# A hybrid decoder layer: 16 of 22 K tiles of the down projection as seven half products, low weight parts last, pairs begun with the weights' sums, nine weight slots

## The chip, the cores and the metric

The kernel runs on one core of a Trainium2 chip. The metric is the device time of one execution in microseconds (us), taken as the median over runs. Engines are named as in the profile: PE (TensorE), DVE (VectorE), ACT (ScalarE), POOL (GpSimd) and SP (SyncE, which issues DMAs).

## The reference, cut to what matters

One layer: a combined input projection, three recurrent branches, a merge, and a SwiGLU feed-forward block (FFN) between RMSNorms. 512 prompt columns and 64 sample columns are computed together, 576 in all, which the kernel holds as two halves of 288. D_MODEL is 1024 (8 tiles of 128), D_FF is 2816 (22 tiles).

```python
h = rmsnorm(x, g_pre_mix)
z = h @ w_in                      # x-branch, gates, S5 input, q, k, v, decays, merge gates
merged = sum(sigmoid(gate_b) * y_b for b in (rglru, s5, gated_delta))
x1 = x + rmsnorm(merged @ w_out, g_post_mix)
h2 = rmsnorm(x1, g_pre_ffn)
act = silu(h2 @ w_gate) * (h2 @ w_up)          # 22 tiles of 128 rows
y = x1 + rmsnorm(act @ w_down, g_post_ffn)
```

## The kernel before

Every product is made in split precision: weight and activation are each kept as a high part (fp32r) and a low part, and one K tile of 128 costs three matmuls of 128x128 by 288 columns: hi by x-hi, hi by x-lo, lo by x-hi. In a GEMM (`mm_part`, lines 210 to 218) these three stand side by side for each K tile; `mm3` takes both halves in turn, weight tile by weight tile, into two accumulators in PSUM.

Weights come from DRAM as raw float32. `wsplit` makes the parts with ACT (a copy to fp32r, L198) and DVE (raw minus hi, L199). `wsplit_dma` makes them with ACT alone (hi, L181, and minus hi, L182) and lets an accumulating DMA, issued by POOL, add the raw weight from DRAM to the low part (L183).

The FFN's gate and up tiles m = 0 to 3 are plain GEMMs. Tiles 4 to 21 are made in pairs, gate pair and up pair for each two tiles, by `pair`: a 2x2 block product with seven half products instead of eight, each a `product` of 4 K tiles (12 matmuls), 84 matmuls a pair. `pair_w` fetches two raw blocks of 512 KB (SP, L1446) and makes from them four sums or differences of weights on DVE (L1452, L1453, L1454, L1459) and seven split weights: three (w0, w1, w6) by DMA, four (w2 to w5) by DVE. DVE also adds the products up (L1482 to L1493) and applies the gate. The activations' sums for this were made before the stage.

`down` multiplies K tiles in groups of four behind the pairs of m = 4, 8, 12 and 16: 8 weights split by DVE, 192 matmuls and 16 evictions (L1519 adds to the accumulator `mx`, the tile `xr`). `down(16, 2)` and a final stage of 4 K tiles end the FFN; the final stage takes half 0 over all 8 output tiles, then half 1, squares and sums for the norm (L1551 eviction, L1557 add), scales (L1561), adds x1 (L1562) and stores y.

What sets the order: every engine runs its instructions in a fixed order, which a scheduler derives from the program's order with priorities (weight preparation is raised by `tc.high_priority`). Buffers recur through pools: raw blocks in 2 + 2 slots, split weights in 4 + 4 slots (`ff_alloc` alternates between the pools `wp` and `sx`), PSUM accumulators in a ring of banks.

```python
def ff_alloc(c):
    wqn[0] += 1
    return two(wp, "wh", "wl")(c) if wqn[0] % 2 else two(sx, "wh", "wl", bufs=4)(c)
```

## Time and profile before

| | |
|---|---|
| median of 3 runs | 1096.17 us (1094.71 to 1105.67) |
| the profiled execution | 1094.42 us |
| its span in the profile | 1092.5 us |
| PE busy | 1041.3 us, 95% |
| DVE busy | 779.0 us, 71% |
| ACT busy | 510.5 us, 47% |
| POOL busy | 167.4 us, 15% |
| mean granted TensorE clock | 0.967 |

The span is what the trace shows between first and last instruction; the execution's time has some 2 us around it. Busy shares are means over stages: the FFN's pairs and down groups run from about 726 to 1052 us. A duration of a matmul (0.3 us) is longer than the step from one to the next, since they are pipelined; the step is read from starts. In a row of the timeline the bracket at the end is the idle time of the engine ahead of the instruction and what ended it.

### The profile page before, as it was taken

Reading aid. Unit: us, or ns where it says so; the run is one execution under the profiler, and the core shown is the slowest. Engines: PE = TensorE matmul, PEld = TensorE weight load, DVE = VectorE, ACT = ScalarE, POOL = GpSimd, SP = SyncE. Lnnn points to the kernel's source line nnn. Section 1 sums busy time; section 2 is a strip of 40 time slices with the busy share of each in tenths; the row PEclk is TensorE's granted clock in tenths of the full one; section 3 lists DMA queues with packets and bytes.
Section 4 is the critical chain, followed back from the end, with each engine's and each line's share of the span. In section 5 each row is a group of like instructions: output and inputs, shape, how many; then the busy total and the mean of one; then the engine's idle time right before and its main releaser. Section 6 shows DMA issues by size and latency. Waiting matters only on the chain.

```text
span 1092.5 us, 20102 instructions
## 1 busy us (share of the span) xinstructions
PE 1041.3 (95%) x7658; PEld 992.8 (91%) x7658; DVE 779.0 (71%) x1893; ACT 510.5 (47%) x1041; POOL 167.4 (15%) x224
## 2 busy tenths in 40 slices
PE   8889898899999999999899999899999999999994
PEld 6788897899999989998699999899999999999994
DVE  7988888646898769844637647874676766857756
ACT  5368667445444423332233535355654635635620
POOL 1132211110120210011000031200211201112124
PEclk9999997699999999999799999999999999999997
DMA  6656664362323133222112622144673736636602
GB/s 210 170 122 143 146 140 98 77 179 88 102 82 107 45 129 119 85 54 97 40 54 74 235 78 75 42 108 118 128 188 75 185 98 136 181 91 145 155 1 87
DMA packets 75138, 122.58 MB, mean 112 GB/s; under 512 B 28186, under 2 KB 36642, under 8 KB 75042
## 3 DMA queue, kind: packets, MB, share of 16 engines
q1 hardware_dynamic: 61938, 97.44, 28.2%
q0 software_dynamic: 13104, 23.86, 13.7%
q8 instruction: 60, 0.98, 0.4%
q14 instruction: 36, 0.29, 0.1%
HBM read 113.03 MB, written 8.24 MB: 111 GB/s over the span
## 4 chain that ended last, share of the span: by engine, by line
PE 73%; DVE 9%; DMA 6%; issue 6%; ACT 3%; POOL 1%; SPq 1%; DVEq 0%; POOLq 0%; ACTq 0%
PE mm L216 13%; PE mm L218 13%; PE mm L217 12%; PE mm L1470 8%; PE mm L1468 8%; PE mm L1469 8%; DMA wl<-in_w_in 2%; DVE wl L199 1%; PE up L1225 1%; DMA wl<-in_w_gate 1%; PE xp L690 1%; DMA wr<-in_w_in 1%; DMA wr<-in_w_gate 1%; PE kp L1036 1%; PE zq L1207 1%
## 5 line engine op out<-in xcount | busy, mean ns | idle before, releaser
L216 PE MATMUL mm<-hh,wh 128*128 128x288 f32 x768 | 231.5, 304 | 3.6 <-DVE u L417 2.3
L198 ACT ACTIVATE wh<-wr 128x512 fp32r<-128x512 f32 x213 | 131.9, 629 | 218.5 <-PE mm L217 118.7
L218 PE MATMUL mm<-hh,wl 128*128 128x288 f32 x768 | 230.3, 301 | 3.5 <-DMA wl<-in_w_in 3.5
L217 PE MATMUL mm<-hl,wh 128*128 128x288 f32 x768 | 230.7, 301 | 0.0
L199 DVE TENSOR_TENSOR wl<-wr,wh 128x512 fp32r<-128x512 f32 x213 | 146.4, 695 | 72.9 <-ACT wh L198 67.2
L216 PEld LDWEIGHTS mm<-hh,wh 128*128 128x128 f32 x768 | 145.9, 191 | 8.4 <-issue 4.8
L218 PEld LDWEIGHTS mm<-hh,wl 128*128 128x128 f32 x768 | 146.2, 191 | 6.8 <-DMA wl<-in_w_in 4.2
L217 PEld LDWEIGHTS mm<-hl,wh 128*128 128x128 f32 x768 | 146.2, 191 | 4.2 <-issue 3.7
L1470 PE MATMUL mm<-fh,wl 128*128 128x288 f32 x352 | 103.8, 295 | 0.0
L1468 PE MATMUL mm<-fh,wh 128*128 128x288 f32 x320 | 94.8, 297 | 0.1
L1469 PE MATMUL mm<-fl,wh 128*128 128x288 f32 x320 | 94.3, 295 | 0.0
L181 ACT ACTIVATE wh<-wr 128x512 fp32r<-128x512 f32 x91 | 56.9, 628 | 78.1 <-PE mm L1469 44.9
L1470 PE MATMUL mm<-hfh,wl 128*128 128x288 f32 x288 | 84.7, 297 | 1.0 <-DMA wl<-in_w_gate 0.9
L1468 PE MATMUL mm<-hfh,wh 128*128 128x288 f32 x288 | 84.8, 295 | 0.0
L1469 PE MATMUL mm<-hfl,wh 128*128 128x288 f32 x288 | 84.8, 295 | 0.0
L216 PE MATMUL mm<-brh,wh 128*128 128x288 f32 x224 | 67.5, 308 | 1.6 <-DVE mg L843 0.9
L217 PE MATMUL mm<-brl,wh 128*128 128x288 f32 x224 | 68.7, 308 | 0.2 <-DVE rho L714 0.2
L218 PE MATMUL mm<-brh,wl 128*128 128x288 f32 x224 | 68.4, 307 | 0.0
L1470 PEld LDWEIGHTS mm<-fh,wl 128*128 128x128 f32 x352 | 66.1, 188 | 0.0
L1469 PE MATMUL mm<-t,wh 128*128 128x288 f32 x216 | 64.0, 297 | 0.0
L1470 PE MATMUL mm<-t,wl 128*128 128x288 f32 x216 | 63.7, 295 | 0.0
L1468 PE MATMUL mm<-t,wh 128*128 128x288 f32 x216 | 63.6, 295 | 0.0
(505 smaller groups left out, 2592.7 us busy)
## 6 DMA issues: line engine op xcount, KB each, us to landing
wr<-in_w_in SPq DMA_DIRECT2D x48, 512.0 KB, 3.5
wr<-in_w_gate SPq DMA_DIRECT2D x22, 512.0 KB, 3.9
wr<-in_w_up SPq DMA_DIRECT2D x22, 512.0 KB, 3.8
wr<-in_w_down SPq DMA_DIRECT2D x20, 512.0 KB, 4.7
wl<-in_w_in POOLq DMA_DIRECT2D x30, 256.0 KB, 5.5
wl<-in_w_gate POOLq DMA_DIRECT2D x27, 256.0 KB, 4.5
wl<-in_w_up POOLq DMA_DIRECT2D x27, 256.0 KB, 4.4
wr<-in_w_out SPq DMA_DIRECT2D x8, 512.0 KB, 3.5
```

Source lines behind the costliest of these rows:

```text
L181: S.activation(hi, raw, AF.Copy)
L198: S.activation(hi, raw, AF.Copy)
L199: (eng or lo_eng()).tensor_tensor(lo, raw, hi.bitcast(F32), op=OP.subtract)
L216: PE.matmul(acc, hi[:, k, :], xh[:, sl], start=k0 + k == 0, stop=False)
L217: PE.matmul(acc, hi[:, k, :], xl[:, sl], start=False, stop=False)
L218: PE.matmul(acc, lo[:, k, :], xh[:, sl], start=False, stop=k0 + k == n - 1)
L690: PE.matmul(xpv[:, b_, :], gm[g // 4][:, g % 4, :], x[:, g, :], start=True, stop=True)
L1036: PE.matmul(kp[:, b], k2[:, sl], kqe[:, :, sl], start=True, stop=True)
L1207: PE.matmul(zqv[:, b], s0[:, b, :], kqe[:, :, c0:c0 + 8], start=True, stop=True)
L1468: PE.matmul(acc, hi[:, k0 + k, :], xh, start=new and k == 0, stop=False, skip_group_check=not new)
L1469: PE.matmul(acc, hi[:, k0 + k, :], xl, start=False, stop=False, skip_group_check=not new)
L1470: PE.matmul(acc, lo[:, k0 + k, :], xh, start=False, stop=k == len(x) - 1, skip_group_check=not new)
```

## The change

1. `product` and the GEMMs (`mm_parts` in place of `mm_part`) issue all hi matmuls of a product first and the matmuls with the low weight part last.
2. `pair` takes its products in the order w2, w3, w0, w4, w1, w5, w6 (before: w0, w2, w3, w4, w1, w5, w6).
3. Split weights have nine slots in place of eight (4 in `wp`, 5 in `sx`).
4. Down of K tiles 0 to 15 is made by `down7`, as seven half products over 2x2 blocks as well: 168 matmuls a group in place of 192, with weights packed on the host (`w_down7`), prepared by `pair_w` as gate and up are, three of seven low parts by DMA. The activations' differences and their splits are made by `down_x0` and `down_x1` (4 differences and 7 splits of 128x576 per group, in place of 4 splits). 28 accumulations a group in place of 16. One term that all pairs of rows share (`ut`) is added once at the end by a broadcast.
5. To make room, x1 is stored to DRAM (`x1d`) and read back for the last step; the activation ring has 3 tiles, one of which lies in the new accumulator tile `fa`, as do the pair's temporaries.
6. The final stage has 6 K tiles (`NL`) in place of 4, and `down(16, 2)` goes.
7. In the last step all adds of squares are on DVE, and half 0's adds of x1 too (before: POOL).

PE's order holds 7042 matmuls before the change and 6946 with it.

```diff
-                PE.matmul(acc, hi[:, k, :], xh[:, sl], start=k0 + k == 0, stop=False)
-                PE.matmul(acc, hi[:, k, :], xl[:, sl], start=False, stop=False)
-                PE.matmul(acc, lo[:, k, :], xh[:, sl], start=False, stop=k0 + k == n - 1)
+    def mm_parts(ps, ws, x, halves, after=None):
+        n = len(x)
+        for lo_part in range(2):
+            k0 = 0
+            for w in ws:
+                for acc, half in zip(ps, halves):
...
+                            if lo_part:
+                                PE.matmul(acc, w[1][:, k, :], xh[:, sl], start=False, stop=k0 + k == n - 1)
+                            else:
+                                PE.matmul(acc, w[0][:, k, :], xh[:, sl], start=k0 + k == 0, stop=False)
+                                PE.matmul(acc, w[0][:, k, :], xl[:, sl], start=False, stop=False)
...
+        SY.dma_start(x1d[:, :, sl], x1t[:, :, sl])
...
-        return two(wp, "wh", "wl")(c) if wqn[0] % 2 else two(sx, "wh", "wl", bufs=4)(c)
+        return two(wp, "wh", "wl")(c) if wqn[0] % 9 in (1, 3, 5, 7) else two(sx, "wh", "wl", bufs=5)(c)
...
         for k, (xh, xl) in enumerate(x):
-            PE.matmul(acc, hi[:, k0 + k, :], xh, start=new and k == 0, stop=False, skip_group_check=not new)
-            PE.matmul(acc, hi[:, k0 + k, :], xl, start=False, stop=False, skip_group_check=not new)
-            PE.matmul(acc, lo[:, k0 + k, :], xh, start=False, stop=k == len(x) - 1, skip_group_check=not new)
+            PE.matmul(acc, hi[:, k0 + k, :], xh, start=new and k == 0, stop=False, skip_group_check=skip)
+            PE.matmul(acc, hi[:, k0 + k, :], xl, start=False, stop=False, skip_group_check=skip)
+        for k, (xh, _) in enumerate(x):
+            PE.matmul(acc, lo[:, k0 + k, :], xh, start=False, stop=k == len(x) - 1 and not more, skip_group_check=skip)
...
+        S.activation(u, product(ws[2], 0, hx[2]), AF.Copy)
+        pz = product(ws[3], 0, hx[3])
         px = product(ws[0], 0, hx[0])
-        S.activation(u, px, AF.Copy)
-        V.tensor_tensor(u, u, product(ws[2], 0, hx[2]), op=OP.add)
-        pz = product(ws[3], 0, hx[3])
+        V.tensor_tensor(u, u, px, op=OP.add)
...
+    def down_x0(k0):
+        t = act2(k0)
+        b11, b12 = (t[:, :, hsl(b)] for b in range(2))
+        dx[0] = fparts(b11)
+        V.tensor_tensor(b11, b12, b11, op=OP.subtract)
+        dx[3] = fparts(b11)
+
+    def down_x1(k0):
+        b11, b12, b21, b22 = quarters(k0)
+        V.tensor_tensor(b12, b22, b12, op=OP.subtract)
+        dx[4] = fparts(b12)
+        dx[5] = fparts(b22)
+        V.tensor_tensor(b22, b22, b11, op=OP.subtract)
+        dx[2] = fparts(b22)
+        dx[1] = fparts(b21)
+        V.tensor_tensor(b21, b21, b22, op=OP.subtract)
+        dx[6] = fparts(b21)
...
+    def down7(k0):
+        c = k0 == 0
+        for g in range(2):
+            ws = pair_w(i["w_down7"], k0 + 2 * g)
+            for e in range(2):
+                p_ = 2 * g + e
+                q = 2 * e
+                u = ut[:, p_, :]
+                c1, c2 = mx[2 * p_], mx[2 * p_ + 1]
+                add_to(u, product(ws[2], q, dx[2]), c)
+                pz = product(ws[3], q, dx[3])
+                add_to(c2[:, hsl(1)], pz, c)
+                px = product(ws[0], q, dx[0])
+                V.tensor_tensor(u, u, px, op=OP.add)
+                pw_ = product(ws[4], q, dx[4])
+                V.tensor_tensor(c2[:, hsl(1)], c2[:, hsl(1)], pw_, op=OP.add)
+                product(ws[1], q, dx[1], px)
+                add_to(c1[:, hsl(0)], px, c)
+                product(ws[5], q, dx[5], pz)
+                add_to(c1[:, hsl(1)], pz, c)
+                product(ws[6], q, dx[6], pw_)
+                add_to(c2[:, hsl(0)], pw_, c)
...
+        if k0 is not None:
+            down_x1(k0)
         pair(i["w_up"], m, lambda a, sl, c: glu_u(t[:, a, sl], c))
...
+        if k0 is not None:
+            down7(k0)
...
-                (V if half and m > 3 else G).tensor_tensor(ss, ss, sq, op=OP.add)
+                V.tensor_tensor(ss, ss, sq, op=OP.add)
...
-            (V if half and m in (3, 5, 7) else G).tensor_tensor(xv, xv, x1[m][:, sl], op=OP.add)
+            (V if half == 0 or m in (3, 5, 7) else G).tensor_tensor(xv, xv, x1[m][:, sl], op=OP.add)
```

In the changed file the matmuls of a GEMM are L226, L227 (hi) and L224 (low), those of a product L1479, L1480 (hi) and L1482 (low); the weights' sums are L1462, L1463, L1464 and L1469; the split by DVE is L200 for weights and L260 for activations; `down7`'s accumulations L1548 to L1565; the last step L1623 (eviction), L1629, L1633, L1634.

**PE where the first pair begins.** Before: the last GEMM of the plain tiles ends (L216 to L218), and the first product takes the weight wh_8682 with its low part wl_8683 from the third matmul on; the names are accumulator<-activation part, weight part.

```order
L218 MATMUL mm_8628<-hfh_7415,wl_8143 128x288
L216 MATMUL mm_8628<-hfh_7417,wh_8142 128x288
L217 MATMUL mm_8628<-hfl_7418,wh_8142 128x288
L218 MATMUL mm_8628<-hfh_7417,wl_8143 128x288
L1468 MATMUL mm_8720<-hfh_7403,wh_8682 128x288
L1469 MATMUL mm_8720<-hfl_7404,wh_8682 128x288
L1470 MATMUL mm_8720<-hfh_7403,wl_8683 128x288
L1468 MATMUL mm_8720<-hfh_7405,wh_8682 128x288
L1469 MATMUL mm_8720<-hfl_7406,wh_8682 128x288
```

Of the change, the same place: the GEMM ends in eight matmuls on low parts, and the first product is on wh_8686, with its two last rows here repeated three times more, eight matmuls without a low part.

```order
L224 MATMUL mm_8616<-hfh_7411,wl_8143 128x288
L224 MATMUL mm_8616<-hfh_7413,wl_8143 128x288
L224 MATMUL mm_8616<-hfh_7415,wl_8143 128x288
L224 MATMUL mm_8616<-hfh_7417,wl_8143 128x288
L1479 MATMUL mm_8713<-t_1450_8424,wh_8686 128x288
L1480 MATMUL mm_8713<-t_1451_8425,wh_8686 128x288
```

The low part has moved behind, and the first weight is another one: wh_8686 is the hi part of w2, wh_8682 and wh_8678 (further on in the change) those of w0.

**DVE around a weights' sum in a cycle of the middle.** Before: L1452 makes the sum ws_10377 from a raw block; L1482 to L1486 evict products, L199 are splits of the weights of the pair before.

```order
L1454 TENSOR_TENSOR wr_10224<-ws_10228,wr_10224 128x512
L1452 TENSOR_TENSOR ws_10377<-wr_10375 128x512
L254 TENSOR_TENSOR fl_10077<-ar_9524,fh_10076 128x576
L1482 TENSOR_TENSOR cu_10121<-cu_10121,mm_10138 128x288
L199 TENSOR_TENSOR wl_10238<-wr_10224,wh_10237 128x512
L1453 TENSOR_TENSOR wr_10375<-wr_10373,wr_10375 128x512
L199 TENSOR_TENSOR wl_10242<-ws_10228,wh_10241 128x512
L1484 TENSOR_TENSOR c_1723_10123<-cu_10121,mm_10152 128x288
L199 TENSOR_TENSOR wl_10246<-wr_10226,wh_10245 128x512
L1486 TENSOR_TENSOR c_1723_10123<-c_1723_10123,mm_10166 128x288
L1459 TENSOR_TENSOR wr_10224<-wr_10224 128x512
L1400 SCALAR_TENSOR_TENSOR ar_10080<-ar_10080,mm_10124 128x288
```

Of the change, the like place, with the sum ws_10001 (L1462); L1538 is a difference of activations, L260 a split of one, L1504 and L1507 evictions of a pair.

```order
L1462 TENSOR_TENSOR ws_10001<-wr_9999 128x512
L1538 TENSOR_TENSOR ar_8206<-ar_8206,fa 128x2x288
L1408 SCALAR_TENSOR_TENSOR ar_8207<-ar_8207,mm_9618 128x288
L200 TENSOR_TENSOR wl_9865<-wr_9851,wh_9864 128x512
L1463 TENSOR_TENSOR wr_9999<-wr_9997,wr_9999 128x512
L1504 TENSOR_TENSOR fa<-fa,mm_9605 128x288
L260 TENSOR_TENSOR fl_9702<-ar_8206,fh_9701 128x576
L1507 TENSOR_TENSOR fa<-fa,mm_9633 128x288
L200 TENSOR_TENSOR wl_9869<-ws_9855,wh_9868 128x512
L260 TENSOR_TENSOR fl_9706<-ar_8206,fh_9705 128x576
L200 TENSOR_TENSOR wl_9873<-wr_9853,wh_9872 128x512
L1497 TENSOR_TENSOR fa<-fa,mm_9781 128x288
```

More rows stand behind the sum that were not there before: differences and splits of 128x576 and, five rows further on, the first eviction of `down7` (L1548, mm_9891).

**DVE in the last half.** Before: an eviction (L1551), the scaling of half 0 (L1561, 8 rows), then evictions and three adds of squares.

```order
L1551 TENSOR_TENSOR xr<-xr,mm_12788 128x288
L1561 SCALAR_TENSOR_TENSOR xr<-xr,par,rows_12710 128x288 x8
L1551 TENSOR_TENSOR xr<-xr,mm_12805 128x288
L1551 TENSOR_TENSOR xr<-xr,mm_12822 128x288
L1551 TENSOR_TENSOR xr<-xr,mm_12839 128x288
L1557 TENSOR_TENSOR fs_12752<-fs_12752,fs_12819 128x288
L1557 TENSOR_TENSOR fs_12752<-fs_12752,fs_12836 128x288
L1557 TENSOR_TENSOR fs_12752<-fs_12752,fs_12853 128x288
L1551 TENSOR_TENSOR xr<-xr,mm_12856 128x288
```

Of the change, the same place: the adds of x1 to half 0 (L1634) stand among the evictions (L1623) and the adds of squares (L1629).

```order
L1633 SCALAR_TENSOR_TENSOR xr<-xr,par,rows_12763 128x288 x8
L1629 TENSOR_TENSOR fs_12811<-fs_12811,fs_12879 128x288
L1634 TENSOR_TENSOR xr<-xr,x_2140_12541 128x288
L1634 TENSOR_TENSOR xr<-xr,x_2141_12542 128x288
L1634 TENSOR_TENSOR xr<-xr,x_2142_12543 128x288
L1634 TENSOR_TENSOR xr<-xr,x_2143_12544 128x288
L1623 TENSOR_TENSOR xr<-xr,mm_12882 128x288
L1634 TENSOR_TENSOR xr<-xr,x_2144_12545 128x288
L1634 TENSOR_TENSOR xr<-xr,x_2145_12546 128x288
L1634 TENSOR_TENSOR xr<-xr,x_2146_12547 128x288
L1634 TENSOR_TENSOR xr<-xr,x_2147_12548 128x288
L1623 TENSOR_TENSOR xr<-xr,mm_12905 128x288
```

Eight rows L1634 have come to DVE ahead of the last evictions.

## Rows read from the trace of the kernel before

**Rows 1.** The page's busy time, share and instructions of each engine.
```profile
PE 1041.3 (95%) x7658; PEld 992.8 (91%) x7658; DVE 779.0 (71%) x1893; ACT 510.5 (47%) x1041; POOL 167.4 (15%) x224
```

**Rows 2.** Busy time of the engines by stretch; the first line names the columns.
```profile
core 0: us, PE busy (x) PEld busy (x) DVE busy (x) ACT busy (x) POOL busy (x), PEclk, DMA share, GB/s
675.00:700.00 25.00, 23.17 (x176) 22.54 (x174) 20.01 (x58) 9.37 (x20) 5.53 (x6) 1.00 0.32 107
175.00:200.00 25.00, 19.66 (x89) 15.48 (x87) 20.46 (x47) 17.10 (x29) 1.04 (x5) 0.60 0.25 54
726.00:1052.00 326.00, 324.91 (x2437) 323.65 (x2437) 225.38 (x423) 169.83 (x309) 46.75 (x55) 1.00 0.55 131
...
792.00:861.00 69.00, 69.00 (x522) 69.00 (x522) 48.20 (x91) 34.59 (x61) 9.55 (x12) 1.00 0.56 133
```

**Rows 3.** DVE's groups, 800 to 1000 us: count, busy us, mean ns, idle before.
```profile
L199 DVE TENSOR_TENSOR wl<-wr,wh 128x512 fp32r<-128x512 f32 x57 | 39.0, 688 | 5.4 <-ACT wh L198 3.7
L1519 DVE TENSOR_TENSOR xr<-xr,mm 128x288 f32<-128x288 f32 x48 | 21.6, 452 | 25.3 <-PE mm L1470 25.2
L254 DVE TENSOR_TENSOR fl<-ar,fh 128x576 fp32r<-128x576 f32 x12 | 9.0, 751 | 0.0
L1452 DVE TENSOR_TENSOR ws<-wr 128x512 f32<-128x512 f32 x12 | 8.3, 693 | 17.7 <-DMA wr<-in_w_gate 12.8 <-DMA wr<-in_w_up 4.8
```

**Rows 4.** PE's timeline, first product of the pairs and two waits (start, us).
```profile
728.36 0.29 PE L1468 MATMUL mm<-hfh,wh 128*128 128x288 f32 x1
...
729.30 0.40 PE L1470 MATMUL mm<-hfh,wl 128*128 128x288 f32 x1 [0.52 <-DMA wl<-in_w_gate]
...
1008.48 0.40 PE L1470 MATMUL mm<-hfh,wl 128*128 128x288 f32 x1 [0.42 <-DMA wl<-in_w_gate]
```

**Rows 5.** PE's timeline in the GEMMs of w_in.
```profile
112.91 0.40 PE L216 MATMUL mm<-hh,wh 128*128 128x288 f32 x1 [0.28 <-ACT pad L453]
...
236.55 0.40 PE L218 MATMUL mm<-hh,wl 128*128 128x288 f32 x1 [1.20 <-DMA wl<-in_w_in]
```

**Rows 6.** DVE's timeline: first sum of weights, an eviction and the next row.
```profile
724.49 0.69 DVE L1452 TENSOR_TENSOR ws<-wr 128x512 f32<-128x512 f32 x1
...
864.19 0.45 DVE L1484 TENSOR_TENSOR c<-cu,mm 128x288 f32<-128x288 f32 x1
864.55 0.69 DVE L199 TENSOR_TENSOR wl<-wr,wh 128x512 fp32r<-128x512 f32 x1
```

**Rows 7.** ACT's timeline, one copy; the page's DMA issues: KB, us to landing.
```profile
845.54 0.63 ACT L181 ACTIVATE wh<-wr 128x512 fp32r<-128x512 f32 x1 [0.95 <-PE mm L1469]
...
wr<-in_w_gate SPq DMA_DIRECT2D x22, 512.0 KB, 3.9
...
wl<-in_w_gate POOLq DMA_DIRECT2D x27, 256.0 KB, 4.5
```

**Rows 8.** PE's and DVE's timelines: release and sum, first and last of 15.
```profile
762.60 0.30 PE L1468 MATMUL mm<-fh,wh 128*128 128x288 f32 x1
...
766.84 0.69 DVE L1452 TENSOR_TENSOR ws<-wr 128x512 f32<-128x512 f32 x1 [5.99 <-DMA wr<-in_w_up]
...
997.23 0.30 PE L1470 MATMUL mm<-hfh,wl 128*128 128x288 f32 x1
...
1005.65 0.69 DVE L1452 TENSOR_TENSOR ws<-wr 128x512 f32<-128x512 f32 x1 [1.80 <-DMA wr<-in_w_up]
```

**Rows 9.** DVE's and PE's timelines at the end.
```profile
1072.98 2.77 DVE L1557 TENSOR_TENSOR fs<-fs,fs 128x288 f32<-128x288 f32 x3
1075.67 0.44 DVE L1551 TENSOR_TENSOR xr<-xr,mm 128x288 f32<-128x288 f32 x1
...
1075.90 0.30 PE L272 MATMUL cps<-con,fs 128*96 128x1 f32 x2 [1.73 <-DVE fs L1557]
...
1085.19 1.88 DVE L1562 TENSOR_TENSOR xr<-xr,x 128x288 f32<-128x288 f32 x3
```

## What the change does to the time: the prediction

> **What bounds the kernel now.** I read the busy shares first: TensorE (PE) is busy 1041.3 of the span of 1092.5 us [rows 1]. [...] So in the FFN a matmul taken away is time taken away, as long as no other engine comes late there. One cycle of that stage (four pairs and one group of down) is the stretch 792 to 861: 522 matmuls in 69.00 us, 0.1322 us each, with DVE at 48.20 us, ACT at 34.59 and POOL at 9.55 [rows 2]. DVE is next in line, 70% busy. The groups of DVE then show what it does there (one 128x512 row takes 0.69 us, an eviction 0.45, a 128x576 row 0.75) and that its idle time stands largely in front of the weights' sums: 17.7 us before 12 of them, released by the raw weights' DMA [rows 3]. The timeline gives the single waits.
>
> The profiled execution took 1094.42 us, 1.75 below the median of the runs (1096.17). The sum is made against 1094.42.
>
> **The change part by part.**
> Matmuls. Four groups of down go from 192 to 168 matmuls each, the rest keeps its count: 96 fewer, at 0.1322 us [rows 2], **-12.7 us**, if nothing is late in their place. [...]
>
> Low parts last. A product that began with hi and lo side by side had to have its low part at the third matmul: PE waited 0.52 us at 729.30 and 0.42 at 1008.48 for one that comes by DMA [rows 4]. Now eight matmuls lie ahead of it, over 1 us: **-0.9**. In the GEMMs of w_in the wait of 1.20 us at 236.55 [rows 5] goes likewise: **-1.2**. Earlier ones lie ahead of the stretch with the clock at 0.60, where PE waits for other engines anyway; I count them at nothing (up to 2 more if that is wrong).
> Against that, in a GEMM of both halves the two accumulators now end four matmuls apart and not twelve, so the first evictions bunch, and a bank of PSUM comes free later for the next GEMM. In the two orders I count 22 places where a bank is wanted less than 2.4 us after its last matmul, against 5. One such wait shows in before, 0.28 us behind an ACT eviction [rows 5]. Bounds: nothing, and 22 x 0.28 = 6. I take **+0.5**, since the evicting engines there are mostly ahead of PE.
>
> Start of the pairs. The first product is now the one on w2, which needs the sum and the two differences and then its split, where w0 needed only a copy. The first sum begins at 724.49 [rows 6]. Six DVE rows and a copy of 0.63 behind it give about 728.8, and PE is ready at about 728.4. With later pairs' first products (traced by hand: 0.5 each for the second pair and the first down) I take **+1.5**, bounds 0 and 3.
>
> The loop of the raw weights. This is the main unknown. A raw block is fetched again only when its last hi copy has a weight slot, and that slot must be freed by PE: ACT's copy (0.63, [rows 7]), SP's issue, the landing (3.9 us at the page's row for gate, [rows 7]), then the sum on DVE. From the freeing matmul to the sum I measured 15 pairs in before: 4.2 us in the first (762.60 to 766.84), 8.4 in the last (997.23 to 1005.65) [rows 8], median 6.2. Behind the sum, on DVE's queue, stand evictions and splits that PE wants. In before nothing is late even at 8.4 us: for the sum ws_10377, whose neighbourhood stands in the order shown with the change, 161 matmuls, 21.3 us, lie between the slot's release and the first matmul that needs what stands behind the sum, and DVE's rows in between take 9.7. In the changed order the like place (ws_10001) has 106 matmuls, 14.0 us, for DVE rows of 9.1: the loop may take 4.9. Summed over the 23 pairs of the changed order by this count, PE is late by 0 at a loop of 4.5 us, 1.2 at 5.5, 4.4 at 6.2, 12.1 at 7.2 and 29.8 at 8.4. I take the median of the measured loops: **+4.4**, bounds 0 and 29.8.
>
> DVE's load. Per cycle come 8 rows of weight sums (8 x 0.69), 7 of 128x576 (4 differences of the activations, 7 splits in place of 4; 7 x 0.75) and 12 evictions (28 for 16; 12 x 0.45) [rows 3]: 16.2 us. 48.20 + 16.2 = 64.4 us in a cycle of 504 matmuls, 66.6 us. It fits, barely: 97% by durations. The durations overlap, though: the eviction at 864.19 has 0.45 and the next row starts 0.36 later [rows 6]; by such steps it is near 90%. Nothing is added for load alone; its price is in the lateness above and in the slow rival below. ACT has 16 more rows a cycle or so and stays near 65%.
>
> DMA'd low parts. Six more accumulating DMAs a cycle (POOL had 12 rows, [rows 2]). Their own loop, copy 0.63, negated copy 0.63, landing 4.5 [rows 7], is 5.8 us; eight weights have slack between 2.8 us and nothing. **+0.8**, bounds 0 and 4. The DMA engines' share is 0.56 there [rows 2], so the transfers, the saved x1 (written and read once) among them, find room.
>
> Tail. In before three adds (L1557) take 2.77 us beside POOL's adds and hold the last eviction to 1075.67; PE waits 1.73 for what follows [rows 9]. Now POOL adds nothing then, but eight adds of half 0 join DVE, 0.63 each by the row at 1085.19 (1.88 for three, [rows 9]), before the last evictions. **-0.5**, bounds -1.2 and +1.4. Two more K tiles in the final stage are matmuls moved, not added. The four broadcast adds lie beside the final weights' products.
>
> Sum: -12.7 - 0.9 - 1.2 + 0.5 + 1.5 + 4.4 + 0.8 - 0.5 = -8.1, so **1086.3 us**.
>
> **The rivals.**
> *Everything is hidden.* Copy and landing alone are 0.63 + 3.9 = 4.5 us [rows 7], and at such a loop nothing is late. Then only the gains stand: 1094.4 - 12.7 - 0.9 - 1.2 - 0.5 = 1079.1. For it: PE was busy 324.91 of 326 us with loops up to 8.4. Against: the margin shrinks from 11.6 to 4.9 us in the example, below the median loop.
> *Slower: DVE's sum blocks its queue.* Place: the weights' sum in the six pairs of a cycle, four of them as before and two new. The sum waits for its DMA and all evictions behind it wait with it. Price: at a loop of 8.4 us 29.8 in place of 4.4, 1111.7. The other way to it: 12 sums waited 17.7 us, 1.5 each [rows 3]; if DVE can't make that up, a cycle needs 64.4 + 6 x 1.5 = 73.4 us against 66.6, over four cycles 27 us, which gives 1109. It decides from the point where the lateness eats all gains, 12.5 us, at a loop of about 7.2 us; two of the measured ends are 4.2 and 8.4. [...]
> *PSUM in the w_in GEMMs.* 22 waits of 0.28: +6 in place of 0.5, about 1092.
> *The clock.* If short waits let the granted clock fall, the FFN would lose more than the waits. At 675 to 700 PE was busy 23.17 of 25.00 us, and the clock stayed at 1.00; at 19.66 it was 0.60 [rows 2]. My 6.5 us of waits spread over 326 us are a smaller share than the idle time of the first of these, so this, with the change doing nothing at all, has little.
>
> **How the numbers follow.** Forecast, 1083 to 1092 with its small bounds: 0.44. All hidden, about 1079: 0.27. PSUM, about 1092: 0.09. Blocked DVE, 1096 and up: 0.17. Clock or no effect: 0.03. A measurement of this kernel can tell about 1%, 11 us. Faster by over 1% is below 1085.2: all of the hidden case, a third of the forecast's, 0.42. Slower by over 1% is above 1107: most of the blocked case, 0.13. Between: 0.45. The range 1078 to 1104 leaves out the far half of the blocked case and the best tenth.
>
> **What would show it.** PE has 96 matmuls less, and a cycle of 504 takes 66.6 us plus idle time in front of the first products of pairs (L1479) and evicted banks; the sum of this idle time in the FFN is about 6.5 us. DVE is above 85% busy in a cycle; its L1462 waits for the raw weights' DMA, 4.2 to 8.4 us after the slot's release. No PE wait for a low part by DMA in the w_in GEMMs. L1629 adds are below 0.86 us each at the tail. I am wrong on the loop if PE idles less than 2 us there, or more than 12; on PSUM if over 3 us of waits for evictions appear before 725; on the clock if a stretch of the FFN is below 1.00.

## The result and the profile after

The changed kernel takes 1108.39 us (median of 20 runs, 1101.93 to 1116.32) against 1095.68 (20 runs, 1092.45 to 1105.67): ratio 1.0112, 95% interval 1.0093 to 1.0131. It is slower by 12.7 us, where 8.1 us faster was forecast. The profiled execution of the changed kernel took 1114.46 us, which is in the upper part of its runs, with a span of 1112.7 for 1092.5.

The page of the changed kernel: busy time by engine, and the granted clock in 40 slices. PE's share fell, DVE's busy time rose from 779.0 [rows 1] to 825.5.

```profile
PE 1043.7 (94%) x7562; PEld 991.2 (89%) x7562; DVE 825.5 (74%) x2002; ACT 538.9 (48%) x1105; POOL 173.2 (16%) x231
...
PEclk9999997899999999997899999999999999989997
```

Where the 20.2 us between the two profiles lie, by the starts of matmuls in PE's timelines:

| part | before | after | difference |
|---|---|---|---|
| up to the last matmul ahead of the first product | 728.24 | 727.50 | -0.7 |
| from there to the last product's last matmul (FFN) | 345.64 | 370.05 | +24.4 |
| from there to the end of the span | 18.65 | 15.15 | -3.5 |

The FFN should have taken 345.6 - 12.7 = 332.9 us with 96 matmuls less, so 37 us came in there. I summed what each row of PE's timeline takes beyond 0.1325 us for each of its matmuls (matmuls of one line that follow without a wait make one row). What is over 0.17 us in a row sums up to 32.4 us (before: 3.4), what is between 0.05 and 0.17 to 9.5 us (before: 1.1); together 37.4 more.

Busy time by stretch, after (columns as in [rows 2]): the FFN window, 69 us of the middle (before a whole cycle [rows 2]; here 460 of its 504 matmuls), a stretch at the start of the pairs with the one after it, a stretch wholly at the lower clock, and one of the worst.

```profile
726.00:1052.00 326.00, 302.66 (x2156) 295.57 (x2155) 257.96 (x497) 192.89 (x361) 66.58 (x77) 0.97 0.67 148
861.00:930.00 69.00, 63.14 (x460) 61.13 (x460) 53.01 (x106) 39.47 (x71) 14.69 (x17) 1.00 0.65 151
...
726.60:731.90 5.30, 1.19 (x10) 0.95 (x8) 5.28 (x11) 4.55 (x11) 1.06 (x2) 1.00 0.34 55
731.90:745.00 13.10, 12.96 (x84) 12.72 (x84) 10.04 (x18) 7.56 (x15) 2.41 (x3) 0.87 0.78 160
...
780.50:783.00 2.50, 2.50 (x12) 2.50 (x12) 2.50 (x5) 0.45 (x2) 0.00 (x0) 0.50 0.43 74
...
980.00:1000.00 20.00, 16.88 (x103) 16.06 (x102) 17.86 (x37) 7.72 (x13) 2.62 (x4) 0.83 0.50 109
```

PE is busy 302.66 of 326 us where it was 324.91 [rows 2], and the clock is no longer 1.00 throughout: behind the stretch in which PE did ten matmuls in 5.30 us it was granted 0.87 on average, a mix of 1.00 and 0.50. DVE isn't full: 257.96 of 326 us, and 53.01 in 69.

What PE waited for most, from 726 to 1095 us, after (total us, times, longest). Before the only such row was 0.9 us for a low part by DMA.

```profile
PE mm L1479 <- ACT wh L199: 6.6, 3, 4.2
PE mm L1482 <- DMA wl<-in_w_down: 5.3, 6, 2.2
PE mm L1479 <- DVE fa L1497: 5.1, 7, 0.9
PE mm L1479 <- DVE fa L1504: 2.1, 2, 1.3
```

What DVE waited for most, 726 to 1052 us, after:

```profile
DVE ws L1462 <- DMA wr<-in_w_down: 18.7, 7, 6.1
DVE ws L1462 <- DMA wr<-in_w_up: 16.5, 6, 4.8
DVE ws L1462 <- DMA wr<-in_w_gate: 8.1, 5, 2.7
DVE wr L1463 <- DMA wr<-in_w_gate: 6.0, 4, 2.2
```

The sums waited 43.3 us in 18 waits for their raw block, and the differences behind them (L1463) another 13; before it was 30.5 in 16, at no cost to PE.

One of these waits, step by step: SP, DVE, ACT and PE timelines, after (start, us, what ended the idle time).

```profile
871.64 0.69 DVE L1462 TENSOR_TENSOR ws<-wr 128x512 f32<-128x512 f32 x1 [2.11 <-DMA wr<-in_w_up]
...
880.71 0.82 SPq L1456 DMA_DIRECT2D wr<-in_w_down  x2
...
881.35 0.45 DVE L1411 TENSOR_TENSOR fa<-fa,mm 128x288 f32<-128x288 f32 x1
887.87 0.69 DVE L1462 TENSOR_TENSOR ws<-wr 128x512 f32<-128x512 f32 x1 [6.07 <-DMA wr<-in_w_down]
888.48 0.45 DVE L1504 TENSOR_TENSOR fa<-fa,mm 128x288 f32<-128x288 f32 x1
888.84 0.68 DVE L1464 TENSOR_TENSOR wr<-ws,wr 128x512 f32<-128x512 f32 x1
...
882.64 0.63 ACT L183 ACTIVATE wl<-wh 128x512 fp32r<-128x512 f32 x1
889.56 0.63 ACT L199 ACTIVATE wh<-wr 128x512 fp32r<-128x512 f32 x1 [6.29 <-DVE wr L1464]
...
890.25 0.40 PE L1479 MATMUL mm<-t,wh 128*128 128x288 f32 x1 [2.08 <-ACT wh L199]
...
902.35 0.29 PE L1479 MATMUL mm<-fh,wh 128*128 128x288 f32 x1
```

SP issues two blocks of a down pair together; 7.16 us later that pair's sum starts. In between DVE stands still for 6.07 us with an eviction (L1504), a difference of weights (L1464) and others behind the sum on its queue, and ACT for 6.29. PE then waits 2.08 us for a weight made from that L1464. This weight does not belong to the down pair: PE's row at 890.25 takes an activation sum `t`, those of the new down are named `fh` and begin at 902.35. By the order of the sums and differences it is the up pair ahead, whose own sum was made at 871.64; its L1464 had nothing left to wait for once ACT's L183 had ended at 883.27. So a sum that was not wanted yet stood in DVE's queue ahead of rows that were.

### The profile page after: what moved, and what is told of

It is laid out like the page before. It is cut to its first block, busy times and chain, and to the rows that moved or that the text cites. A ratio compares the mean times of both kernels' runs of the same rounds, so it can differ in the third digit from the quotient of the medians.

```text
span 1112.7 us, 20158 instructions
## 1 busy us (share of the span) xinstructions
PE 1043.7 (94%) x7562; PEld 991.2 (89%) x7562; DVE 825.5 (74%) x2002; ACT 538.9 (48%) x1105; POOL 173.2 (16%) x231
## 4 chain that ended last, share of the span: by engine, by line
PE 58%; DVE 17%; DMA 14%; issue 6%; ACT 3%; POOL 1%; SPq 1%; DVEq 0%; POOLq 0%; ACTq 0%
PE mm L226 12%; PE mm L224 12%; PE mm L227 12%; PE mm L1479 4%; PE mm L1482 4%; PE mm L1480 4%; DMA wr<-in_w_down 3%; DVE wl L200 3%; DMA wr<-in_w_up 3%; DMA wl<-in_w_down 2%; DMA wr<-in_w_gate 1%; ACT wh L182 1%; PE up L1231 1%; POOL wl L184 1%; DMA wl<-in_w_gate 1%
## 5 line engine op out<-in xcount | busy, mean ns | idle before, releaser
L199 ACT ACTIVATE wh<-wr 128x512 fp32r<-128x512 f32 x205 | 126.2, 628 | 204.9 <-PE mm L227 87.3
L226 PE MATMUL mm<-hh,wh 128*128 128x288 f32 x768 | 214.3, 304 | 2.9 <-DVE u L423 2.3
L227 PE MATMUL mm<-hl,wh 128*128 128x288 f32 x768 | 211.5, 301 | 0.0
L200 DVE TENSOR_TENSOR wl<-wr,wh 128x512 fp32r<-128x512 f32 x205 | 141.0, 696 | 41.9 <-ACT wh L199 21.7
L226 PEld LDWEIGHTS mm<-hh,wh 128*128 128x128 f32 x768 | 146.8, 192 | 9.6 <-issue 7.4
L227 PEld LDWEIGHTS mm<-hl,wh 128*128 128x128 f32 x768 | 146.6, 192 | 2.0 <-issue 1.7
L224 PE MATMUL mm<-hh,wl 128*128 128x288 f32 x768 | 125.6, 304 | 1.4 <-DMA wl<-in_w_in 1.4
L224 PEld LDWEIGHTS mm<-hh,wl 128*128 128x128 f32 x768 | 109.3, 191 | 5.0 <-issue 2.2
L1479 PE MATMUL mm<-hfh,wh 128*128 128x288 f32 x288 | 81.5, 305 | 5.9 <-DVE fa L1497 5.1
L1479 PE MATMUL mm<-fh,wh 128*128 128x288 f32 x288 | 80.5, 302 | 3.9 <-DVE fa L1507 1.4
L1480 PE MATMUL mm<-fl,wh 128*128 128x288 f32 x288 | 80.8, 300 | 0.0
L1480 PE MATMUL mm<-hfl,wh 128*128 128x288 f32 x288 | 80.5, 300 | 0.0
L183 ACT ACTIVATE wl<-wh 128x512 fp32r<-128x512 f32 x115 | 71.6, 626 | 7.0 <-PE mm L224 3.8
L1482 PE MATMUL mm<-fh,wl 128*128 128x288 f32 x320 | 66.4, 301 | 5.6 <-DMA wl<-in_w_down 5.3
L1479 PE MATMUL mm<-t,wh 128*128 128x288 f32 x216 | 61.3, 304 | 7.9 <-ACT wh L199 6.6
L226 PE MATMUL mm<-brh,wh 128*128 128x288 f32 x224 | 64.3, 311 | 3.3 <-ACT gt L835 2.0
L227 PE MATMUL mm<-brl,wh 128*128 128x288 f32 x224 | 63.1, 306 | 0.2 <-DVE brl L260 0.2
L1479 PEld LDWEIGHTS mm<-hfh,wh 128*128 128x128 f32 x288 | 55.5, 193 | 8.4 <-DVE fa L1497 6.9
L1480 PE MATMUL mm<-t,wh 128*128 128x288 f32 x216 | 61.0, 303 | 0.0
L1479 PEld LDWEIGHTS mm<-fh,wh 128*128 128x128 f32 x288 | 54.5, 191 | 5.2 <-DVE fa L1507 1.7
L1482 PEld LDWEIGHTS mm<-fh,wl 128*128 128x128 f32 x320 | 51.0, 192 | 7.4 <-DMA wl<-in_w_down 7.0
```

The source lines that it names most:

```text
L183: S.activation(lo, hi.bitcast(F32), AF.Copy, scale=-1.0)
L199: S.activation(hi, raw, AF.Copy)
L200: (eng or lo_eng()).tensor_tensor(lo, raw, hi.bitcast(F32), op=OP.subtract)
L224: PE.matmul(acc, w[1][:, k, :], xh[:, sl], start=False, stop=k0 + k == n - 1)
L226: PE.matmul(acc, w[0][:, k, :], xh[:, sl], start=k0 + k == 0, stop=False)
L227: PE.matmul(acc, w[0][:, k, :], xl[:, sl], start=False, stop=False)
```

## The experiments

Two theories at first. R, the loop of the raw weights: what is late is the landing of the raw blocks, and DVE's queue carries it to PE. L, DVE has too much work. Besides, O: the new order of the products makes PE need the sum's weights 12 matmuls earlier. The ratios are those to the kernel before; the changed kernel has 1.0112. FFN is the length of that part in the profile, gaps are what PE's rows take beyond their matmuls by over 0.17 us (as above), sums the waits of the weights' sums for their DMA, all in us. They are those of one profiled execution, which can lie off the median of the kernel's runs: 6.1 us above it for the changed kernel, 5.4 below for low parts side by side, 8.5 below for five slots, old order, side by side. Between kernels the ratio decides.

| kernel | ratio (95%) | FFN | gaps | sums |
|---|---|---|---|---|
| before | 1 | 345.6 | 3.4 | 30.5 |
| changed | 1.0112 (1.0093 to 1.0131) | 370.1 | 32.4 | 43.3 |
| five raw slots | 1.0035 (1.0008 to 1.0061) | 359.4 | 24.5 | 40.5 |
| old order of pairs | 0.9983 (0.9958 to 1.0008) | 352.8 | 20.7 | 26.4 |
| low parts side by side | 1.0085 (1.0057 to 1.0112) | 358.5 | 22.6 | 24.3 |
| plain down | 0.9982 (0.9958 to 1.0006) | 345.8 | 4.4 | 37.5 |
| five slots, old order | 1.0017 (0.9985 to 1.0049) | 353.5 | 19.7 | 35.7 |
| the same, old order in down too | 0.9995 (0.9967 to 1.0023) | 351.9 | 18.9 | 38.5 |
| five slots, old order, side by side | 1.0079 (1.0045 to 1.0113) | 352.3 | 20.4 | 31.6 |
| less work for DVE | 1.0184 (1.0135 to 1.0233) | 369.2 | 34.2 | 52.0 |
| small raw blocks | 0.994 (0.992 to 0.996) | 344.1 | 13.8 | 29.6 |
| raw blocks swapped | 1.0112 (1.0082 to 1.0143) | 367.3 | 32.7 | 47.1 |
| old order, blocks swapped | 1.0000 (0.9978 to 1.0022) | 351.5 | 20.4 | 24.8 |
| old order, low parts by DVE | 1.0015 (0.9994 to 1.0037) | 354.5 | 23.3 | 23.2 |
| old order, small raw blocks | 0.9889 (0.9854 to 0.9925) | 340.0 | 10.1 | 28.6 |
| old order, differences on POOL | 1.0101 (1.0071 to 1.0131) | 365.9 | 31.5 | 32.6 |
| before, low parts last | 0.997 (0.9949 to 0.9991) | 346.1 | 4.7 | 31.3 |
| the same, last step's adds on DVE | 0.9991 (0.997 to 1.0012) | 347.6 | 6.0 | 30.8 |

**A fifth raw slot.** On the changed kernel:

```diff
-        return (wp if rawn[0] % 2 else sx).tile([128, KT, 128], F32, name=nm("wr"), tag="wr", bufs=2)
+        return (wp.tile([128, KT, 128], F32, name=nm("wr"), tag="wr", bufs=2) if rawn[0] % 5 in (1, 3)
+                else sx.tile([128, KT, 128], F32, name=nm("wr"), tag="wr", bufs=3))
...
-            sq = sx.tile([128, NH], F32, name=nm("fs"), tag="c0" if m else "c1")
+            sq = fa[:, 6 + m % 2, hsl(m // 2 % 2)] if m else fa[:, 4 + half, hsl(0)]
```

> The changed kernel with a fifth slot for raw weight blocks (4 KB per partition; the squares of the last step move into the tile fa to make room). Theory R, the loop of the raw weights: a block can be fetched one block earlier, so the waits of the weights' sums for their DMA (43.3 us in 18 waits between 726 and 1052 us of the changed kernel) fall to half or less, PE's idle time in the FFN (31 us of steps over 0.3 us) too, and the time is 1088 to 1098 us. Theory L, DVE has too much work: the sums come earlier but DVE ends no earlier, time within 4 us of 1108. Theory O, the order of the products: the same, 1104 to 1110.

1099.04 us, a gain of some 8 us. The direction is R's, the size is not: the sums' waits went from 43.3 to 40.5 us only. Why isn't shown: the order of DVE is another one, but the sums do not stand further forward in it (counted by the evictions ahead of each, 0.8 later on average).

**The old order of the pairs' products.** On the changed kernel:

```diff
-        S.activation(u, product(ws[2], 0, hx[2]), AF.Copy)
-        pz = product(ws[3], 0, hx[3])
         px = product(ws[0], 0, hx[0])
-        V.tensor_tensor(u, u, px, op=OP.add)
+        S.activation(u, px, AF.Copy)
+        V.tensor_tensor(u, u, product(ws[2], 0, hx[2]), op=OP.add)
+        pz = product(ws[3], 0, hx[3])
```

> The changed kernel with the pairs' products in the old order, w0 first, then w2, w3 (gate and up only; the new down keeps its own order). Theory O: the product on w2 needs six rows of DVE behind the sum while w0 needs one copy, so 18 pairs win back up to 12 matmuls (1.6 us) each; the time falls by 10 us or more, to 1085 to 1098. Theory R: the evictions behind a late sum are late as before, only the first product of a pair is not; 1101 to 1106. Theory L: no change, 1106 to 1110.

1093.88 us: the order of the products was worth 14 us. The 96 matmuls are still not seen; 20.7 us of gaps are left.

**Low part side by side, in the products.** On the changed kernel, the low matmul goes back into the loop over K:

```diff
             PE.matmul(acc, hi[:, k0 + k, :], xl, start=False, stop=False, skip_group_check=skip)
-        for k, (xh, _) in enumerate(x):
             PE.matmul(acc, lo[:, k0 + k, :], xh, start=False, stop=k == len(x) - 1 and not more, skip_group_check=skip)
```

> The changed kernel with the low part of a weight again right behind its two hi matmuls, in the products of the FFN alone (the GEMMs keep low last). Theories R and L: low parts are wanted 6 matmuls earlier on average, the third matmul of a product waits for its DMA (5.3 us of such waits in the changed kernel, growing by 0.5 to 1 us in each of the 12 to 20 late products): 1110 to 1122. Rival, low last itself costs time since a hi slot comes free no earlier and the end of a product hangs on the low part: 1100 to 1107.

1104.53 us, not slower. PE waited 7.9 us for low parts of down by DMA (5.3 before this edit), and 4.0 for low parts by DVE, but less for evictions: the scheduler's order came out another one, with 24.3 us of sums' waits. So this says nothing for or against low last by itself.

**Plain down.** On the kernel before: `mm_parts` for `mm_part`, the low parts of a product in a loop of their own, and the pairs' new order.

```diff
-            PE.matmul(acc, lo[:, k0 + k, :], xh, start=False, stop=k == len(x) - 1, skip_group_check=not new)
+        for k, (xh, _) in enumerate(x):
+            PE.matmul(acc, lo[:, k0 + k, :], xh, start=False, stop=k == len(x) - 1, skip_group_check=not new)
...
-        px = product(ws[0], 0, hx[0])
-        S.activation(u, px, AF.Copy)
-        V.tensor_tensor(u, u, product(ws[2], 0, hx[2]), op=OP.add)
+        S.activation(u, product(ws[2], 0, hx[2]), AF.Copy)
         pz = product(ws[3], 0, hx[3])
+        px = product(ws[0], 0, hx[0])
+        V.tensor_tensor(u, u, px, op=OP.add)
```

> The kernel before with low parts last everywhere and with the pairs' new order, but with plain down, eight slots, and the old last step. If the new down (its DVE rows, its DMA'd low parts, its two more pairs a cycle in the raw loop) carries the loss: 1090 to 1097. If the order of the products or low parts last carry half of it: 1100 to 1106. Theory O alone: 1106 or more.

1093.96 us. With plain down the new order costs nothing: 4.4 us of gaps, though the sums wait 37.5 us. A plain group puts 192 matmuls with no raw sum between two pairs; the new down puts 168 and two more sums there. So the new down is needed for the loss; which part of it (the sums, its low parts by DMA, DVE's rows) this run doesn't tell.

**Both remedies, and variants.** The edits of the first two experiments together, five raw slots and the old order:

> Five raw slots and the old order of the pairs' products together. One wait, two ways round it (R and O are the same late sum): the gains overlap, 1088 to 1094 us. Two separate losses (the late first product, and the evictions behind the sum): they add, 9 + 14 us below 1108, 1083 to 1087. Theory L, what is left of PE's idle time in the FFN (15 us in either run) is DVE's load: not below 1091.

1095.19 us: no sum of two gains. That fits one wait with two ways round it, though the time is a little above the range given for that, and L's bound (not below 1091) holds as well. To this, w0 first in `down7` too:

```diff
-                add_to(u, product(ws[2], q, dx[2]), c)
-                pz = product(ws[3], q, dx[3])
-                add_to(c2[:, hsl(1)], pz, c)
                 px = product(ws[0], q, dx[0])
-                V.tensor_tensor(u, u, px, op=OP.add)
+                add_to(u, px, c)
+                p2 = product(ws[2], q, dx[2])
+                V.tensor_tensor(u, u, p2, op=OP.add)
+                pz = product(ws[3], q, dx[3])
+                add_to(c2[:, hsl(1)], pz, c)
```

> As the last, with the products of the new down in the order w0, w2, w3 too (8 pairs of weights, 16 times). If the first product on a weight made from the sum is what is late, 8 more pairs win up to 1.5 us each: 4 to 10 us below the run with the pairs alone. If what is left is DVE's load or the low parts by DMA: within 3 us of it. Rival: the low part of w0 comes by DMA and is now wanted first, 2 to 5 us slower.

1093.64 us, within 3 us of the run without it: the order inside the new down isn't what is left, unless its gain and the earlier need of w0's low part cancel. And five slots and the old order with the low part side by side, by the edit shown above:

> As the first of this set, with the low part of a weight right behind its hi matmuls in the products. With w0 first its low part by DMA is wanted at the third matmul: where this loop is tight, 5 to 10 us slower. If low last is worth nothing in the FFN (the run with the new order and side by side was 4 us faster than the changed kernel): within 3 us or faster.

1104.06 us, 9 us slower by the medians, as the first theory gave it: with w0 first its low part by DMA is wanted third. The profile cannot show the loss, since its execution took 1095.6 us, the shortest of ten; in it PE waited 6.2 us for low parts of gate, 3.6 of down and 3.0 of up, against 2.4 of gate and 1.9 of down without this edit. So low last seems to earn its place here; the cause is argued from these waits.

**Less work for DVE.** On the changed kernel: low parts of `dx` are made for the first group only.

```diff
-        hi, lo = (fp.tile([128, 2, NH], F32R, name=nm(t), tag=t) for t in ("fh", "fl"))
-        split(src, hi, lo)
+        hi = fp.tile([128, 2, NH], F32R, name=nm("fh"), tag="fh")
+        if j in flo:
+            lo = flo[j]
+            S.activation(hi, src, AF.Copy)
+        else:
+            lo = flo[j] = fp.tile([128, 2, NH], F32R, name=nm("fl"), tag="fl")
+            split(src, hi, lo)
```

> The changed kernel, with the low parts of the new down's seven activation tiles made for the first group only and used again in the other three: 21 rows of 0.75 us, 15.8 us, leave DVE; the results of the down projection are not the reference's. Theory L: PE's idle time in the FFN falls by about what DVE saves, the time to 1090 to 1097. Theory R and O: the sums wait for their DMA as before, the evictions behind them come at most a few rows earlier, 1102 to 1107.

1114.98 us, slower by 7 than the changed kernel, outside what either theory gave. PE's waits of that kernel:

```profile
PE mm L1482 <- DVE wl L200: 13.6, 7, 2.8
PE mm L1482 <- DMA wl<-in_w_down: 5.0, 3, 2.0
```

With 15.8 us less on DVE, low parts that DVE makes came late, and the sums now waited 52.0 us. The sums do not stand further forward in DVE's order (0.4 evictions later on average), so why this cost 7 us stays open. It speaks against L as a bound by the amount of work.

**Small raw blocks.** On the changed kernel, four fixed raw tiles, and:

```diff
-            SY.dma_start(r[a], src[m + a])
+            if rawn[0] <= 4:
+                SY.dma_start(r[a], src[m + a])
+            else:
+                SY.dma_start(r[a][:, 0::4, :], src[m + a][:, 0::4, :])
```

> The changed kernel with four fixed raw tiles, of which each pair after the first two fetches only a quarter (K tiles 0 and 4 of 8, 128 KB for 512); the sums run over what else stands in the tile, so results are not the reference's. The order of the work and the rows of DVE stay as they are, only the landing is shorter (issue to sum 5.7 us median, 8.5 at most, in the changed kernel). Theory R: sums wait for about half as long, PE's idle time in the FFN (32 us of gaps) falls to 10 or less, 1080 to 1092 us. If the waits come from ACT's copies and the order alone, not from the landing: 1100 or more.

1090.05 us, 18 us below the changed kernel with the same number of rows on every engine. The DMA issues of that kernel in the window (KB, us to landing) show the quarter blocks beside the full ones of the last groups:

```profile
wr<-in_w_down SPq DMA_DIRECT2D x6, 512.0 KB, 5.3
...
wr<-in_w_down SPq DMA_DIRECT2D x16, 128.0 KB, 2.7
wr<-in_w_gate SPq DMA_DIRECT2D x16, 128.0 KB, 2.8
wr<-in_w_up SPq DMA_DIRECT2D x16, 128.0 KB, 3.6
```

So the landing of the raw blocks is shown as the main cause: from issue to a sum that waited it took 3.9 us at the median for 5.7 (longest 6.2 for 8.5), and the gaps fell from 32.4 to 13.8 us. DVE's order is nearly the same, no sum has more than one eviction more or less ahead of it. The low parts by DMA land earlier too in this run (4.2 to 4.5 us for 4.9 to 5.7), so that a part of the gain is theirs: PE's own waits for them fell from 5.3 to 2.1 us.

**Raw blocks in the other order**, on the changed kernel and on the one with the old order:

```diff
         for a in range(2):
             r.append(ff_raw())
+        for a in (1, 0):
             SY.dma_start(r[a], src[m + a])
```

> The changed kernel with the two raw blocks of a pair fetched in the other order: the sum needs only the second block, which now goes first on SP's queue. Theory R (the sum waits for the landing of two blocks issued together, 7 to 8.5 us): the sum starts some 2 us earlier in half the pairs, 1098 to 1104. Rival, the slot of the second block comes free last, so that both blocks are issued later: no change or slower, 1106 to 1114.

> The changed kernel with the pairs' products in the old order and the second raw block fetched first. With w0 first, the first block is what the first product needs and the second what the second needs: by R 1 to 5 us below the run with the old order alone (1093.9); by the rival (slot freed last) 2 to 8 us above.

1108.39 and 1096.39 us: nothing gained. That fits the rival, in which both blocks are issued only when the last slot is free (the two at 880.71 above go out together).

**Low parts of the new down by DVE**, on the kernel with the old order:

```diff
-            w0 = wsplit_dma(a11, d11, ff_alloc)
+            dn = src is i["w_down7"]
+            w0 = wsplit(a11, ff_alloc, eng=V) if dn else wsplit_dma(a11, d11, ff_alloc)
...
-            w1 = wsplit_dma(a12, d12, ff_alloc)
+            w1 = wsplit(a12, ff_alloc, eng=V) if dn else wsplit_dma(a12, d12, ff_alloc)
...
-        return [w0, w1, w2, w3, w4, wsplit(a12, ff_alloc, eng=V), wsplit_dma(a22, d22, ff_alloc)]
+        w5 = wsplit(a12, ff_alloc, eng=V)
+        return [w0, w1, w2, w3, w4, w5, wsplit(a22, ff_alloc, eng=V) if dn else wsplit_dma(a22, d22, ff_alloc)]
```

> The changed kernel with the pairs' products in the old order, and the three low parts of a pair of the new down that came by accumulating DMA made by DVE: 24 DMAs of 256 KB fewer, 24 rows of 0.69 us (16.6 us) more on DVE. Theory D, what is left of PE's idle time (20 us of gaps) comes from the low parts by DMA and their share of the DMA engines (0.69 against 0.55): 1086 to 1092. Theory L, DVE's load: 1097 or more. Neither: 1092 to 1096.

1097.64 us, 3 to 4 above the old order alone, and the gaps 23.3 for 20.7. That lies in the range of theory L, by 0.6 us; a gain from 24 DMAs less and a loss from 24 rows more may also hide each other here. The DMA engines' share fell to 0.56, and still evictions of the pairs (L1500) held PE, as the second line shows:

```profile
726.00:1052.00 326.00, 308.38 (x2279) 304.32 (x2280) 281.57 (x542) 183.25 (x344) 45.27 (x53) 0.99 0.56 138
...
PE mm L1481 <- DVE fa L1500: 9.4, 6, 2.4
```

So the share of the DMA engines by itself isn't what is left; the next run decides about L.

**What is left with the old order.** The same small raw blocks on the kernel with the old order:

> The changed kernel with the pairs' products in the old order, and four fixed raw tiles of which only a quarter is fetched anew for each pair (results of the FFN are not the reference's). If what is left in the kernel with the old order is again the landing of the raw blocks: gaps in the FFN fall below 8 us, 1078 to 1085. If it is DVE's load, or the low parts by DMA (9 us of PE's waits there): 1088 to 1094.

1084.43 us: a further 10 us, and PE busy 319.45 of 326 us:

```profile
726.00:1052.00 326.00, 319.45 (x2388) 316.96 (x2389) 273.58 (x540) 200.00 (x375) 66.58 (x77) 1.00 0.53 99
```

DVE does the same rows in less time, so it is busier here than in the changed kernel, 273.58 of 326 us for 257.96, and PE hardly waits. Its waits for low parts by DMA fell from 9.4 us (old order alone) to 4.1. That is the clearest row against L. With the landing out of the way the 96 matmuls less show: the FFN takes 340.0 us for 345.6, with 6.7 us more of gaps than before. The gaps are 10.1 us, above the 8 that I had given.

Then the differences on POOL, with full blocks, in all four of `down_x0` and `down_x1`:

```diff
-        V.tensor_tensor(b11, b12, b11, op=OP.subtract)
+        G.tensor_tensor(b11, b12, b11, op=OP.subtract)
```

> The changed kernel with the pairs' products in the old order and the four differences of activations of each group of the new down on POOL instead of DVE: 16 rows of 0.75 us, 12 us, leave DVE, and POOL takes more than twice as long for each. If DVE's load is what is left: 1086 to 1091. If it is the landing: 1092 to 1097, and slower still if the splits behind the differences now come late.

1107.71 us. A difference takes 1.5 to 1.7 us on POOL (means by line) for 0.75 on DVE in the changed kernel, and the splits behind it came late: evictions of the pairs (L1498) held PE for 5.1 us (3.2 in the old order alone), those of the new down (L1565) for 4.4, and low parts by DMA for 10.3, which is hardly more than the 9.4 of the old order alone.

**The parts without the new down.** The kernel before with low parts last, which is the run with plain down without its second piece; then with the last step's adds on DVE as well:

```diff
-                (V if half and m > 3 else G).tensor_tensor(ss, ss, sq, op=OP.add)
+                V.tensor_tensor(ss, ss, sq, op=OP.add)
...
-            (V if half and m in (3, 5, 7) else G).tensor_tensor(xv, xv, x1[m][:, sl], op=OP.add)
+            (V if half == 0 or m in (3, 5, 7) else G).tensor_tensor(xv, xv, x1[m][:, sl], op=OP.add)
```

> The kernel before with low parts last in all products and GEMMs, and nothing else. By the terms of the sum (-0.9 and -1.2 for waits on low parts, +0.5 for banks of PSUM): 1.6 us below before, 1093 to 1096. If banks that come free late are dearer (22 places at 0.28 us): 3 to 6 us above before.

1092.29 us, ratio 0.997 (0.9949 to 0.9991): the shortest time of the kernels here that compute the whole layer, and the only one of them whose interval lies below the kernel before; the intervals of the old order and of plain down overlap it.

> The kernel before with low parts last everywhere and the adds of the last step moved to DVE as in the changed kernel (squares, and x1 of half 0); no new down, old order of the pairs, eight slots. If the last step's 3.3 us between the two profiles come from these adds: 2 to 4 us below low parts last alone (ratio 0.997), so 0.993 to 0.995 of before. If they come from elsewhere (the run to run spread of the last stores): 0.996 to 0.999.

1095.37 us, ratio 0.9991 (0.997 to 1.0012), so the adds of the last step give nothing that can be told, and the gain of low parts last alone is not firm either; the shorter end in the profile of the changed kernel isn't explained by the adds.

## Why the prediction was wrong, point by point

**The sum of the matmuls, -12.7: right, and hidden.** PE has 96 matmuls less. The 0.1322 us that I took for each is the step in a cycle of the FFN's pairs and a group of down, a stage with PE busy 324.91 of 326.00 us [rows 2]. The 96 show only where the raw blocks land in time (1084.43 us).

**The loop of the raw weights, +4.4: the step that failed.** The mechanism and the place were right, the size was not. I put the median of 15 loops of the kernel before, 6.2 us, into a sum that is bent: 4.4 at 6.2, 12.1 at 7.2, 29.8 at 8.4. Two things are wrong with that. First, the long loops cost most. In the changed kernel six of 18 sums that waited start 6.85 to 8.51 us after their blocks' issue, and a copy of 0.63 [rows 7] lies ahead of the issue; before, too, four of 16 had started 7.2 to 7.7 us after one. Second, the loops did not stay those of before. From issue to a sum that waited it took 5.7 us at the median for 4.0 before, with the DMA engines' share at 0.67 for 0.55 [rows 2]; I had let the transfers "find room" and put nothing for this. What the loop cost is measured by the small blocks, which bring this stretch back to 3.9 us: 18 us, in place of 4.4. That the gaps grew by 29.0 us, nearly the 29.8 that my count gave for 8.4, is luck. Only a third of these loops was that long, and the 29.0 hold other waits, the 5.3 us for low parts by DMA among them; I did not count again with the loops of the changed kernel.

**The rival of the blocked queue, 0.17.** This is what came: 1109 to 1112 was its price, 1108.4 the result, in the far half of this case that my range left out; that the price fits so well is luck, as above. That the rows behind a waiting sum wait with it I had taken as given; the changed kernel shows it by the 6.07 us for which DVE stood still ahead of 887.87: behind the sum stood an eviction (L1504, 888.48) whose product PE had finished by 886.6. What PE then waited for was not this eviction but a weight of the pair ahead, whose difference stood behind the sum too. The second way to it, DVE's load, was wrong: DVE's busy time rose by 46.5 us and not by 4 x 16.2 = 65 (some 7 of the difference are the 16 evictions of `down(16, 2)`, which went), in the 69 us of the middle it was 77% busy and not above 85%, and the run with DVE at 273.58 of 326 us is the fastest of all.

**Start of the pairs, +1.5 (0 to 3).** Too small. PE waited 4.17 us for the first weight, with the first sum at 726.62 for 724.49 [rows 6], itself behind its DMA by 2.74 us. The old order gives back 14 us over all pairs; I had traced three pairs and taken the others as free, though w2 hangs on the sum in each. These 14 us and the 18 of the small blocks overlap, since both together give 24.

**The clock, 0.03.** I gave it as all or nothing. It came as a share: steps at the lower level (0.50; 0.24 us a matmul for 0.13) cost 8.4 us of the 37.4, behind stretches in which PE waited (0.87 on average at 731.9 to 745, 0.83 at 980 to 1000). So these waits cost more than their own length; behind the one of 2.08 us ahead of 890.25 the clock stayed at 1.00.

**Low parts by DMA, +0.8 (0 to 4).** Too small: PE waited 5.3 us for low parts of down. Their landing rose from 4.4 to 5.7 us for up, with a DMA share of 0.67 for 0.55 [rows 2].

**Low parts last, -2.1, and PSUM, +0.5.** Alone it measured 3.3 us below before, between 1.0 and 5.6 by the interval; the terms said 1.6. Waits on ACT's evictions ahead of 725 us (L780, L835) are 2.6 us in three, after 1.3 in three before, those on DVE's (L849) 2.2 after 2.5: together 1.0 us more. The waits for low parts in the GEMMs of w_in are down from 3.5 to 1.4 us, where I had expected none to be left.

**Tail, -0.5.** 3.5 us in the profiles, but the adds alone gave nothing in the last run. Of the 3.5, 2.1 us lie behind the last add (5.45 us to the end of the span before, 3.35 after). The run with low parts of the new down by DVE has the changed last step and again 5.45 there, so these 2.1 us are not the adds'. The other 1.4 us are open.

What stays open: each edit made the scheduler order the engines anew, so hardly a run changes one wait alone, and the less loaded DVE at 1114.98 isn't explained. The landing's share was measured with the same rows and nearly the same order. Why the landing took longer in the changed kernel wasn't taken apart, nor were the 10 us of gaps that even the small blocks left. And no run moved the sums back in DVE's queue, behind the rows that PE wants first.

## What to carry to other kernels

When a change takes slack out of a loop, price the loop at its long half and not at its median (by my count the lateness is nil up to the slack and grows with every us behind it), and ask whether the change itself lengthens the loop: here issue to sum went from 4.0 to 5.7 us. Look for what stands behind an instruction that waits for a DMA: here the sum that waited 6.07 us held up the eviction and the differences behind it on DVE. Here moving the consumer that needs it (the old order, 14 us) or shortening the transfer (18 us) was worth more than taking 15.8 us of work from the engine, which made the kernel 7 us slower. Ask, too, whether the matmuls that go were the cover of such a loop: here the 96 that went showed only with small raw blocks (with the old order, an FFN of 340.0 us for 345.6).

## What the runs showed of the hardware

Where two blocks of 512 KB went out within 1.5 us of one another, a sum that waited for them started 4.0 to 8.5 us after the first issue (ten times in the changed kernel). The median landing of a 512 KB block there was 4.2 (gate) to 5.6 us (down), that of 128 KB 2.7 to 3.6 in the kernel with small blocks: a quarter of the bytes took 0.5 to 0.7 of the time.

In the FFN of the changed kernel the granted clock fell to 0.50 five times, behind waits of PE of 0.7 to 4.2 us (behind one of 2.15 us ahead of 779.66 it was 0.50 from 780.5 to 783 with PE busy all the time), and stayed at 1.00 behind one of 2.08 us ahead of 890.25. In the kernel before, with PE busy 324.91 of 326.00 us, it had been 1.00 [rows 2]. Means such as 0.83 and 0.87 are of stretches with both levels.
